# Weight sums of a block's first Strassen pass: accumulating DMAs in place of GpSimd adds, two operands with the other sign

## The chip, the cores and the metric

The kernel runs on one core of a Trainium2 chip. The metric is the device time of one execution in microseconds (us). Of the kernel before, three runs are at hand: 2923.96, 2926.63 and 2928.53 us, the median being 2926.63 us. The engines are called by the profile's names: PE (TensorE; PEld its weight loads), DVE (VectorE), ACT (ScalarE), POOL (GpSimd) and SP (SyncE, which issues DMAs).

## The reference, cut to what matters

One layer of a streaming encoder: an input projection, two token mixers (a gMLP chunk gate and a Mamba-2 SSD), and an output projection.

```python
def mixer_layer(x, ...):
    h = rms_norm(x, norm_in_w) @ w_in                 # 4096 (+64) tokens x 1024 @ 1024 x 5648
    u, v, g, z, xbc, dt_raw = jnp.split(h, SPLITS, axis=-1)
    a_out, vn = gmlp_branch(u, v, g, ...)
    b_out, h_last, new_conv = mamba_branch(z, xbc, dt_raw, ...)
    y = x + jnp.concatenate([a_out, b_out], axis=-1) @ w_out
```

The change concerns only the weights `w_in` of the first product, `h = norm(x) @ w_in`.

## The kernel before, in words

The 4096 tokens are worked through in blocks of 768 tokens (five of them, numbers 0 to 4) and a last block of 256 tokens with the 64 sample tokens. Blocks 0 to 4 compute the input projection by one level of Strassen's scheme (Winograd's form): a pair of 128-column slices of `w_in` is a unit, its 1024 x 256 weights are four quarters a11, a12 (one column slice, two halves of the rows) and a21, a22 (the other), and seven products q of combined quarters with combined activations give the unit's output. They are made in the order 1, 2, 4, 6, 7, 5, 3. Besides two v units (for v and dt) there are 18 units: c0 to c5 (for the convolution), then u0, g0, u1, g1, ... u3, g3, then z0 to z3, the last two interleaved.

Every operand of a product is split into a rounded part and a remainder (`hi` and `lo`), and three matmuls of each pair of 128-row tiles are summed, so a product is 12 matmuls of 384 columns (`products`, L1150 to L1152).

In block 0 the weight operands are made from the raw weights by `make`, written to DRAM (`wop_...`), and read back by `load` in blocks 1 to 4. So the sums of quarters are taken in block 0 alone. In `make(u, q, ts)`:

- L397, before product 1: a21 = a21 + a22.
- L403 and L404, every product: ACT copies the operand to `hi` (rounding), and DVE or POOL (`on_pool`: q = 4, 5, 3 of most units) takes `lo = src - hi`. L408 and L410 then send both to DRAM by SP's queue.
- L419, after product 1: a11 = a21 - a11, which is the operand of product 6.
- L421, after product 2: a12 = a12 - a11, the operand of product 3.
- L423, after product 4: a22 = a22 - a11, the operand of product 7.
- The operand of product 5 is a21.

These four sums are POOL instructions (128 x 512), save those of the units z2 and z3, which are DVE's; those of the two v units are DVE's (L412 to L414) and, for a12, POOL's (L415).

Raw weights lie in three buffers `wx`, one for (a11, a12) and one for (a21, a22) of a unit: `fetch` (L335) loads the second pair of the next unit early, and its first pair (a11, a12) into the buffer that is released when product 5 of the present unit has been made; the pair after that when product 3 has. Operands go to four buffers `w` that PE empties, so `ahead` runs up to four products ahead of PE. Each engine takes its instructions in the order that the scheduler of the program gave it, and each waits for semaphores.

`add_up` (L1159 on) adds each product into the four output quarters as it comes, on DVE, or on ACT where it only copies.

Between the projections of a block, its SSD steps, convolution and gates run on DVE, ACT and PE (`L910`, `L945`, `L1205` to `L1211` and others), on the same queues.

Of the kernel before, what the change touches and what calls it, by code (L numbers as in the profile page):

```python
# [10 lines left out]
AF = mybir.ActivationFunctionType  # L11
ALU = mybir.AluOpType
# [5 lines left out]
ADD, SUB = ALU.add, ALU.subtract  # L18
# [33 lines left out]
def hybrid_step_kernel(  # L52
# [30 lines left out]
    act, dve, pool, pe, sp = nc.scalar, nc.vector, nc.gpsimd, nc.tensor, nc.sync  # L83
# [44 lines left out]
    def phase1(p2):  # L128
# [141 lines left out]
        class Operands:  # L270
# [117 lines left out]
            def make(self, u, q, ts):  # L388


                v = u[0] == "v"
                n = 4 * WGD if v else 4 * P
                r = self.raw[u]

                eng = dve if u in (("z", 2), ("z", 3)) else pool
                if q == 1 and not v:
                    eng.tensor_tensor(r["a21"], r["a21"], r["a22"], ADD)  # L397
                src = r[{1: "a11", 2: "a12", 4: "a22", 6: "a11", 7: "a22", 5: "a21", 3: "a12"}[q]]
                if v:
                    hi, lo = ts  # L400
                else:
                    hi, lo = ts[0][:, :n], ts[0][:, n : 2 * n]
                act.copy(hi, src)  # L403
                (pool if q in self.on_pool[u[0]] else dve).tensor_tensor(lo, src, hi.bitcast(F32), SUB)  # L404
                k = ORDER.index(q)
                if v:
                    for i, x in enumerate((hi, lo)):
                        sp.dma_start(wops[u][(2 * k + i) * P : (2 * k + i + 1) * P, :], x.bitcast(F32))  # L408
                else:
                    sp.dma_start(wops[u][k * P : (k + 1) * P, :], ts[0][:, : 2 * n].bitcast(F32))  # L410
                if v and q == 4:
                    dve.tensor_tensor(r["a21"], r["a21"], r["a22"], ADD)  # L412
                    dve.tensor_tensor(r["a11"], r["a21"], r["a11"], SUB)
                    dve.tensor_tensor(r["a22"], r["a22"], r["a11"], SUB)  # L414
                    pool.tensor_tensor(r["a12"], r["a12"], r["a11"], SUB)  # L415
                elif v:
                    pass
                elif q == 1:
                    eng.tensor_tensor(r["a11"], r["a21"], r["a11"], SUB)  # L419
                elif q == 2:  # L420
                    eng.tensor_tensor(r["a12"], r["a12"], r["a11"], SUB)  # L421
                elif q == 4:
                    eng.tensor_tensor(r["a22"], r["a22"], r["a11"], SUB)  # L423
                if q in ((5, 3) if not v else (7, 5) if u[1] else (6, 7, 5)):
                    self.free += 1
                if q == 3:
                    del self.raw[u]
                self.fetch()
                return hi, lo
# [651 lines left out]
        class Strassen(Block):  # L1081
# [77 lines left out]
            def add_up(self, q, b, cs, hold=None):  # L1159

                c11, c12, c21, c22 = cs
                if q == 1:
                    act.copy(c12, b)
                elif q == 2:
                    dve.tensor_tensor(c11, b, c12, ADD)
                elif q == 4:
                    if hold is None:
                        act.copy(c21, b)
                    else:
                        hold.append(b)  # L1170
                elif q == 6:
                    dve.tensor_tensor(c12, b, c12, ADD)
                elif q == 7:
                    dve.tensor_tensor(c22, b, c12, ADD)  # L1174
                    dve.tensor_tensor(c21, hold.pop() if hold else c21, c22, ADD)
                elif q == 5:
                    dve.tensor_tensor(c22, b, c22, ADD)  # L1177
                    dve.tensor_tensor(c12, b, c12, ADD)
                else:
                    dve.tensor_tensor(c12, b, c12, ADD)  # L1180

# [679 lines left out]
```

## Time and profile before

| | |
|---|---|
| runs | 2923.96, 2926.63, 2928.53 us |
| the profiled execution | 2926.66 us, its span 2924.9 us |
| PE, PEld busy | 2800.6 us (96%), 2607.1 us (89%) |
| DVE, ACT, POOL busy | 2184.0 us (75%), 1283.8 us (44%), 670.2 us (23%) |
| granted TensorE clock, mean | 0.983 |
| DMA | 689.18 MB, mean 236 GB/s |

The span is the time from the first to the last instruction. Busy PE means that a matmul was under way. In a list of groups, a row is one kind of instruction: line, engine, operation, output<-input, shapes, count, then busy us and mean ns of one, then the idle time of that engine just before it and what ended it. In a timeline a row is: start in us, length in us, instruction, count, and in brackets the idle time before it and what ended that.

### The profile page before, as it was taken

Reading aid. Unit: us, or ns where it says so; the run is one execution under the profiler, and the core shown is the slowest. Engines: PE = TensorE matmul, PEld = TensorE weight load, DVE = VectorE, ACT = ScalarE, POOL = GpSimd, SP = SyncE. Lnnn points to the kernel's source line nnn. Section 1 sums busy time; section 2 is a strip of 40 time slices with the busy share of each in tenths; the row PEclk is TensorE's granted clock in tenths of the full one; section 3 lists DMA queues with packets and bytes.
Section 4 is the critical chain, followed back from the end, with each engine's and each line's share of the span. In section 5 each row is a group of like instructions: output and inputs, shape, how many; then the busy total and the mean of one; then the engine's idle time right before and its main releaser. Section 6 shows DMA issues by size and latency. Waiting matters only on the chain. (4 is left out here: it accounts for less than half of the span.)

```text
span 2924.9 us, 45556 instructions
## 1 busy us (share of the span) xinstructions
PE 2800.6 (96%) x16917; PEld 2607.1 (89%) x16917; DVE 2184.0 (75%) x3613; ACT 1283.8 (44%) x2415; POOL 670.2 (23%) x537
## 2 busy tenths in 40 slices
PE   5988998999999999999999999999999899989998
PEld 5887888999999999999999999999898688878886
DVE  7988888768757777676777666775666766698887
ACT  4366654245623365431664315663275222253332
POOL 1464443210012100031000211001311433353432
PEclk8998999999999999999999999999999899999999
DMA  8766777877788777886777877778776545544453
GB/s 284 270 243 228 248 281 282 305 229 236 243 312 278 233 235 245 285 309 218 253 243 266 288 252 238 235 251 281 232 257 224 160 163 171 173 158 166 166 173 112
DMA packets 310373, 689.18 MB, mean 236 GB/s; under 512 B 30264, under 2 KB 156936, under 8 KB 310152
## 3 DMA queue, kind: packets, MB, share of 16 engines
q1 hardware_dynamic: 309112, 686.26, 70.2%
q8 instruction: 135, 2.21, 0.3%
q14 instruction: 86, 0.70, 0.1%
q10 hardware_dynamic: 1040, 0.00, 0.0%
HBM read 535.43 MB, written 150.75 MB: 235 GB/s over the span
## 5 line engine op out<-in xcount | busy, mean ns | idle before, releaser
L1150 PE MATMUL mm<-hop,w 128*128 128x384 f32 x1656 | 577.8, 349 | 14.9 <-ACT w L403 6.9
L1152 PE MATMUL mm<-hop,w 128*128 128x384 f32 x1656 | 563.7, 340 | 11.8 <-POOL w L404 7.1
L1151 PE MATMUL mm<-hop,w 128*128 128x384 f32 x1656 | 563.0, 340 | 0.0
L1658 PE MATMUL pa<-wlo,oh 128*128 128x512 f32 (+1 forms) x928 | 366.3, 395 | 13.4 <-DVE wlo L1612 13.4
L1659 PE MATMUL pa<-whi,ol 128*128 128x512 f32 (+1 forms) x928 | 364.4, 393 | 3.5 <-DVE ol L1620 3.5
L1657 PE MATMUL pa<-whi,oh 128*128 128x512 f32 (+1 forms) x928 | 364.4, 393 | 2.6 <-ACT whi L1611 1.4
L1150 PEld LDWEIGHTS mm<-hop,w 128*128 128x128 f32 x1656 | 314.3, 190 | 24.0 <-ACT w L403 10.8
L1152 PEld LDWEIGHTS mm<-hop,w 128*128 128x128 f32 x1656 | 313.9, 190 | 16.5 <-POOL w L404 9.1
L1151 PEld LDWEIGHTS mm<-hop,w 128*128 128x128 f32 x1656 | 314.3, 190 | 4.0 <-issue 2.4
L1150 PE MATMUL mm<-hop,wy 128*128 128x384 f32 x864 | 297.0, 344 | 1.8 <-DVE arena L1174 1.8
L1151 PE MATMUL mm<-hop,wy 128*128 128x384 f32 x864 | 292.2, 338 | 0.0
L1152 PE MATMUL mm<-hop,wy 128*128 128x384 f32 x864 | 291.7, 338 | 0.0
L1658 PEld LDWEIGHTS pa<-wlo,oh 128*128 128x128 f32 (+1 forms) x928 | 174.3, 188 | 57.6 <-DVE wlo L1612 19.4
L1659 PEld LDWEIGHTS pa<-whi,ol 128*128 128x128 f32 (+1 forms) x928 | 174.7, 188 | 42.5 <-DVE ol L1620 4.2
L1657 PEld LDWEIGHTS pa<-whi,oh 128*128 128x128 f32 (+1 forms) x928 | 174.2, 188 | 42.2 <-ACT whi L1611 1.8
L1110 PE MATMUL mm<-w,hop 128*128 128x260 f32 x552 | 160.4, 292 | 14.4 <-ACT w L403 12.2
L910 ACT ACTIVATE acb<-acb,acu 128x128 f32<-128x128 f32 (+1 forms) x528 | 166.6, 389 | 0.6
L1150 PEld LDWEIGHTS mm<-hop,wy 128*128 128x128 f32 x864 | 162.4, 188 | 3.3 <-DVE arena L1174 2.4
L1151 PEld LDWEIGHTS mm<-hop,wy 128*128 128x128 f32 x864 | 162.5, 188 | 1.3
L1152 PEld LDWEIGHTS mm<-hop,wy 128*128 128x128 f32 x864 | 162.2, 188 | 0.3
L1112 PE MATMUL mm<-w,hop 128*128 128x260 f32 x552 | 158.1, 287 | 0.0
L1202 ACT ACTIVATE arena<-cvr,prm 128x768 f32<-128x768 f32 x60 | 61.5, 1027 | 192.6 <-DVE cvr L1177 152.9
(337 smaller groups left out, 6345.1 us busy)
## 6 DMA issues: line engine op xcount, KB each, us to landing
w<-wop_c SPq DMA_DIRECT2D x114, 512.0 KB, 4.3
w<-wop_v SPq DMA_DIRECT2D x84, 520.0 KB, 4.9
w<-wop_u SPq DMA_DIRECT2D x76, 512.0 KB, 4.3
w<-wop_g SPq DMA_DIRECT2D x76, 512.0 KB, 4.4
w<-wop_z SPq DMA_DIRECT2D x76, 512.0 KB, 5.3
wy<-wop_c SPq DMA_DIRECT2D x72, 512.0 KB, 4.4
acb<-acd SPq DMA_DIRECT2D x66, 512.0 KB, 5.3
raw<-ab SPq DMA_DIRECT2D x64, 512.0 KB, 4.4
```

The lines of the kernel that those rows point to most:

```text
L910: act.activation(M[:L, i, :L], M[:L, i, :L], AF.Relu, bias=self.acu[:L, ci, h0 + i : h0 + i + 1])
L1110: pe.matmul(pv, a, hi[:, j, :], start=(j == 0), stop=False)
L1112: pe.matmul(pv, b, hi[:, j, :], start=False, stop=(j == 3))
L1150: pe.matmul(b, hi[:, j, :], thi[:, j, :], start=j == 0, stop=False)
L1151: pe.matmul(b, hi[:, j, :], tlo[:, j, :], start=False, stop=False)
L1152: pe.matmul(b, lo[:, j, :], thi[:, j, :], start=False, stop=j == 3)
L1202: act.activation(o, raw[:, 3 : 3 + TS], AF.Identity, bias=prm[:, CB + c : CB + c + 1], scale=cw(3))
L1657: pe.matmul(b, x[0][:, j, :], hi, start=first, stop=False)
L1658: pe.matmul(b, x[0][:, j, :], lo, start=False, stop=False)
L1659: pe.matmul(b, x[1][:, j, :], hi, start=False, stop=last)
```

## The change

The sums of the 18 units become DMAs that POOL issues with an accumulation, `r[a] = r[a] + r[b]`, from SBUF to SBUF. Since such a DMA adds only, a21 + a22 is multiplied by -1 on ACT, in place, right after it is formed. Then a11 + a21 is the negative of what L419 made, so the operands of products 6 (a11) and 5 (a21) have the other sign, while a12 + a11 and a22 + a11 are what L421 and L423 made. `add_up` subtracts products 6 and 5. The v units take the same signs on DVE, and POOL's sum of theirs moves to DVE.

```diff
-                eng = dve if u in (("z", 2), ("z", 3)) else pool
+                add = lambda a, b: pool.dma_start(r[a], r[b], accum_op=ADD)
                 if q == 1 and not v:
-                    eng.tensor_tensor(r["a21"], r["a21"], r["a22"], ADD)
+                    add("a21", "a22")
+                    act.activation(r["a21"], r["a21"], AF.Copy, scale=-1.0)
...
                 if v and q == 4:
-                    dve.tensor_tensor(r["a21"], r["a21"], r["a22"], ADD)
-                    dve.tensor_tensor(r["a11"], r["a21"], r["a11"], SUB)
-                    dve.tensor_tensor(r["a22"], r["a22"], r["a11"], SUB)
-                    pool.tensor_tensor(r["a12"], r["a12"], r["a11"], SUB)
+                    dve.scalar_tensor_tensor(r["a21"], r["a21"], -1.0, r["a22"], ALU.mult, SUB)
+                    for a, b in (("a11", "a21"), ("a22", "a11"), ("a12", "a11")):
+                        dve.tensor_tensor(r[a], r[a], r[b], ADD)
                 elif v:
                     pass
                 elif q == 1:
-                    eng.tensor_tensor(r["a11"], r["a21"], r["a11"], SUB)
+                    add("a11", "a21")
                 elif q == 2:
-                    eng.tensor_tensor(r["a12"], r["a12"], r["a11"], SUB)
+                    add("a12", "a11")
                 elif q == 4:
-                    eng.tensor_tensor(r["a22"], r["a22"], r["a11"], SUB)
+                    add("a22", "a11")
...
                 elif q == 6:
-                    dve.tensor_tensor(c12, b, c12, ADD)
+                    dve.tensor_tensor(c12, c12, b, SUB)
...
                 elif q == 5:
-                    dve.tensor_tensor(c22, b, c22, ADD)
-                    dve.tensor_tensor(c12, b, c12, ADD)
+                    dve.tensor_tensor(c22, c22, b, SUB)
+                    dve.tensor_tensor(c12, c12, b, SUB)
```

In the changed kernel all four adds of a unit stand on L394, and lines after L415 are numbered one lower. The scheduler orders the instructions of each engine anew. Two places show it.

POOL's queue for the last convolution unit, c5, before (`wx_1891` holds a11 and a12, `wx_1751` a21 and a22 of c5; `wx_1916` holds a21 and a22 of the next unit):

```order
L419 TENSOR_TENSOR wx_1891<-wx_1751,wx_1891 128x512
L404 TENSOR_TENSOR w_1983<-wx_1751,w_1983 128x512
L421 TENSOR_TENSOR wx_1891<-wx_1891 128x512
L423 TENSOR_TENSOR wx_1751<-wx_1751,wx_1891 128x512
L397 TENSOR_TENSOR wx_1916<-wx_1916 128x512
L1212 COPY carp_145<-cvr_1847 128x3
```

and POOL's queue for the same unit in the changed kernel (`wx_1896` holds a11 and a12, `wx_1755` a21 and a22, `wx_1921` those of the next unit):

```order
L394 DMA wx_1896<-wx_1755 128x512
L404 TENSOR_TENSOR w_1989<-wx_1755,w_1989 128x512
L394 DMA wx_1921<-wx_1921 128x512
L394 DMA wx_1896<-wx_1896 128x512
L394 DMA wx_1755<-wx_1896 128x512
```

The a21 sum of the next unit has moved ahead of the a12 and a22 sums of the present one; those two wait for the landing of the first DMA, and the a22 sum is issued after the a12 sum.

ACT's queue in the changed kernel, around the copies for products 6, 7, 5 and 3 of unit c5 (L403 are the `hi` copies; L1201, L1212, L944, L1162 and L875 are other work of ACT):

```order
L1162 COPY cvr_2014<-mm_2018 128x384
L875 COPY bt_2245<-ss_2193 128x256
L403 CAST w_2009<-wx_1896 128x512
L944 ACTIVATE arena_155<-arena_155,prm_76 128x128 x2
L397 ACTIVATE wx_1921<-wx_1921 128x512
L403 CAST w_2031<-wx_1755 128x512
L403 CAST w_2052<-wx_1755 128x512
L1212 ACT_TABLE_LOAD
L1212 ACTIVATE arena_155<-arena_155 128x768
L403 CAST w_2075<-wx_1896 128x512
L1212 ACTIVATE arena_155<-arena_155 128x768
L1201 ACTIVATE arena_155<-cvr_2016,prm_76 128x768
```

The multiplication by -1 (L397) stands between the copies for products 6 and 7, so it is ahead of the copy that waits for the a22 sum.

## Rows read from the trace of the kernel before

**Rows 1.** Busy time by stretch: the 18 units of block 0, those of block 1.

```profile
core 0: us, PE busy (x) PEld busy (x) DVE busy (x) ACT busy (x) POOL busy (x), PEclk, DMA share, GB/s
103.70:501.60 397.90, 346.62 (x2014) 324.40 (x2013) 331.93 (x476) 227.19 (x426) 191.44 (x144) 0.95 0.71 253
566.40:884.60 318.20, 317.03 (x2005) 308.67 (x2003) 230.13 (x394) 154.75 (x301) 25.31 (x32) 1.00 0.78 258
```

**Rows 2.** Waits of ACT from 100 to 500 us: us in total, times, longest.

```profile
ACT w L403 <- DMA wx<-in_w_in_dram: 30.0, 7, 8.2
ACT w L403 <- POOL wx L423: 28.0, 8, 4.9
```

**Rows 3.** Timeline of POOL, unit c5.

```profile
210.02 1.68 POOL L419 TENSOR_TENSOR wx<-wx 128x512 f32<-128x512 f32 x1 [1.86 <-DVE w L404]
211.66 2.01 POOL L404 TENSOR_TENSOR w<-wx,w 128x512 fp32r<-128x512 f32 x1
...
215.33 2.01 POOL L423 TENSOR_TENSOR wx<-wx 128x512 f32<-128x512 f32 x1
```

**Rows 4.** Timeline of ACT and of SP's queue, unit c5 to the next.

```profile
208.62 1.64 ACT L403 CAST w<-wx 128x512 fp32r<-128x512 f32 x3
...
217.37 0.62 ACT L403 CAST w<-wx 128x512 fp32r<-128x512 f32 x1 [2.93 <-POOL wx L423]
...
229.11 1.64 ACT L403 CAST w<-wx 128x512 fp32r<-128x512 f32 x3
...
222.69 1.17 SPq L335 DMA_DIRECT2D wx<-in_w_in_dram  x1
```

**Rows 5.** Timeline of POOL and ACT in unit g0.

```profile
258.74 1.30 POOL L423 TENSOR_TENSOR wx<-wx 128x512 f32<-128x512 f32 x1
...
265.03 0.60 ACT L403 CAST w<-wx 128x512 fp32r<-128x512 f32 x1
```

**Rows 6.** Groups of POOL from 100 to 500 us (of four adds, the first and the last).

```profile
L404 POOL TENSOR_TENSOR w<-wx,w 128x512 fp32r<-128x512 f32 x49 | 78.5, 1606 | 98.9 <-ACT w L403 94.8 <-issue 3.5 <-POOL w L404 0.5
L423 POOL TENSOR_TENSOR wx<-wx 128x512 f32<-128x512 f32 x16 | 25.0, 1562 | 0.5
...
L397 POOL TENSOR_TENSOR wx<-wx 128x512 f32<-128x512 f32 x15 | 22.4, 1492 | 25.4 <-DMA wx<-in_w_in_dram 25.2
```

**Rows 7.** Groups of DVE from 100 to 500 us.

```profile
L404 DVE TENSOR_TENSOR w<-wx,w 128x512 fp32r<-128x512 f32 x73 | 64.9, 897 | 34.2 <-ACT w L403 33.7
L1211 DVE SCALAR_TENSOR_TENSOR arena<-cvr,prm,arena 128x768 f32<-128x768 f32 x12 | 18.1, 1509 | 0.1
L1017 DVE TENSOR_TENSOR S<-S,dte 128x512 f32<-128x512 f32 x12 | 13.1, 1090 | 0.0
L397 DVE TENSOR_TENSOR wx<-wx 128x512 f32<-128x512 f32 x2 | 2.5, 1231 | 0.0
```

**Rows 8.** Groups of DVE from 566 to 884 us, in block 1.

```profile
L1211 DVE SCALAR_TENSOR_TENSOR arena<-cvr,prm,arena 128x768 f32<-128x768 f32 x12 | 12.2, 1014 | 0.2
L1017 DVE TENSOR_TENSOR S<-S,dte 128x512 f32<-128x512 f32 x12 | 8.2, 683 | 0.0
```

**Rows 9.** Instructions on tile w, 100 to 500 us: duration in ns, min/median/max.

```profile
L403 ACT CAST w<-wx x122: 600/615/627, 99.5 to 486.7; 128x512 fp32r<-128x512 f32 x122
L404 DVE TENSOR_TENSOR w<-wx,w x73: 673/692/1939, 100.2 to 485.9; 128x512 fp32r<-128x512 f32 x73
L410 SPq DMA_DIRECT2D wop_c<-w x42: 319/320/1282, 100.9 to 224.3; - x42
```

**Rows 10.** DMAs from 100 to 500 us: packets; count, KB each, median us to landing.

```profile
DMA packets 58067, 101.36 MB, mean 253 GB/s; under 512 B 3096, under 2 KB 36984, under 8 KB 58038
...
wop_c<-w SPq DMA_DIRECT2D x42, 512.0 KB, 2.6
wx<-in_w_in_dram SPq DMA_DIRECT2D x32, 512.0 KB, 5.5
wop_u<-w SPq DMA_DIRECT2D x28, 512.0 KB, 3.5
```

## The prediction

> **What bounds the kernel now.** I read the busy time by stretch first. PE is busy nearly always over the whole span, so only a stretch in which it isn't can give time back. The 18 units of block 0 take 397.9 us for 2014 matmuls, those of block 1 318.2 us for 2005 [rows 1]: 80 us are lost in block 0, at a granted clock of 0.95 against 1.00. In the stretch that loses time the weight operands are made: ACT, DVE and POOL all have more to do, and POOL is busy 191 us instead of 25. The sums that the change moves lie there and nowhere else, so 80 us is all that it could win.
>
> Then the waits of ACT in that stretch. Its copies of operands wait 28.0 us in 8 units for POOL's a22 sum (L423), and 30.0 us in 7 units for raw weights [rows 2]. These waits form a cycle, which the timelines of unit c5 show: the copy for product 1 starts at 208.62, as soon as a11 and a12 have landed [rows 4]; POOL starts the a11 sum at 210.02 and ends the a22 sum at 217.34, with the remainder of product 4 and the a12 sum between [rows 3]; at 217.37 ACT copies for product 7 [rows 4]; product 5 releases the buffer, SP issues the next a11 and a12 at 222.69, and the next unit's first copy starts at 229.11 [rows 4]. That is 20.5 us per unit, of which POOL's link is 7.32 us. PE empties only four operands ahead of this.
>
> Not every unit hangs on that link. In g0 the a22 sum ends at 260.04 and its copy comes at 265.03 [rows 5]: 5.0 us of slack, since ACT's queue holds other work first.
>
> Last, the groups. POOL's four adds of a unit cost 25.0 to 22.4 us a group (four groups, about 95 us together), its remainders 78.5 us [rows 6]. DVE's instructions with two inputs in SBUF are slow beside them: 1509 and 1090 ns for forms that take 1014 and 683 ns in block 1 [rows 7, 8], and the remainder on DVE takes 897 ns in the mean where its median is 692 [rows 7, 9].
>
> **The change part by part.** The sum is made against the profiled execution, 2926.66 us (span 2924.9), which is the median of the runs (2926.63) to 0.03 us.
>
> *POOL's adds go.* DVE loses time to POOL of 73 x 0.205 = 15.0 us on the remainders, 12 x 0.495 = 5.9 us on L1211 and 12 x 0.407 = 4.9 us on L1017, 25.8 us in all [rows 7 to 9]. The adds are 95 of the 95 + 78.5 us in which POOL works on two such inputs [rows 6], so 55% of it, 14 us, goes. The remainders on POOL stay, and the rest of the delay with them. DVE's own eight adds for z2 and z3 go too: at 0.69 to 1.23 us each [rows 7, 9], 8 us. Against that stand two sums of the v units that POOL did and DVE now does, at about twice that form's length, 2.5 us. DVE gets 14 + 8 - 2.5 = 20 us back. Between 0 (all of it hidden under the cycle) and 20 us reach the path; I take half, **-10 us**, since ACT, DVE and POOL take turns in the cycle but much of DVE's work is beside it.
>
> *The DMAs come.* Let X be the time from POOL's issue of such a DMA to its landing and x what POOL spends on an issue. In place of POOL's link stand: a11 (X), the issue of a12 (x), a22 (X), so 2X + x; product 4's remainder and the next unit's a21 sum run on POOL during the first flight. No row shows an accumulating DMA. The nearest rows are stores of operands from SBUF: 512 KB landing after 2.6 and 3.5 us [rows 10]. The new ones move 256 KB but read source and destination, about as many bytes read. The lower end is 2.6, the upper the loads' 5.5 us [rows 10]. For x the ends are SP's issue, 0.32 us [rows 9], and a short POOL add, 1.3 us [rows 5]. I take X = 3.5 and x = 0.8, the longer store and the middle: 7.8 us for 7.32, +0.5 us in each of the 8 units that wait there, **+4 us**. In the ten others the slack of 5.0 us covers it. The link's ends are 5.5 us (-1.8 x 8 = -14 us) and 12.3 us (+5.0 x 8 = +40 us). POOL's link also waits now for ACT's multiplication, which was finished during the unit before.
>
> By the Trainium skill (DMA: Bandwidth & Descriptors, "Anatomy of one DMA - SWDGE (gpsimd) path") a DMA issued by GpSimd takes about 2.0 us plus its bytes over 436 GB/s, which estimates 2.6 us for 256 KB. With that as X the link would be 6.0 us and this term -10 us instead of +4. No run here shows it, and it counts neither the second read nor the traffic beside it, so it stays out of my sum.
>
> *The multiplication by -1 on ACT*: 18 x 0.615 us = 11 us at the length of a copy of that shape [rows 9]. It waits for the landing of the a21 sum, and behind it in ACT's queue stands the copy for product 7. That one waits for a DMA issued two issues later, so the cover is the a22 flight: **0**. Were the loads of a21 and a22 late, POOL would hold a12 and a22 behind the a21 sum, ACT the copy, and up to 11 us show.
>
> *The 16 DMA engines*: 72 DMAs of 256 KB are 18.9 MB beside 101.4 MB in the stretch [rows 10], at a busy share of 0.71 [rows 1]. The loads of a11 and a12, 5.5 us, are on every unit's cycle. I put 0.2 us on most of 18, **+3 us**; from 0 to 5.5 x 0.19 x 18 = 18 us if loads stretch as the bytes do.
>
> *The signs*: a subtraction instead of an addition of the same shapes in `add_up`: 0; it is the same DVE instruction.
>
> Sum: -10 + 4 + 0 + 3 = -3 us: 2923 us, **no change** by 0.2% (5.9 us), which is about what a measurement of this kernel can tell. This case by itself spans 2910 to 2935.
>
> **The rivals.**
>
> *Slower: the DMA's latency takes the place of POOL's add on the cycle.* Place: from the a11 sum to the copy for product 7, twice per unit. For it: two flights in series stand where four short adds stood, and loads take 5.5 us under this traffic. Against: stores take 2.6. With the relief of -10 and +3, 8 x (2X + 0.8 - 7.32) passes 7 us at X = 3.7 and makes the kernel slower by 0.2% at X = 4.1. At X = 5.5 and x = 1.3 it is +40 - 10 + 3 = +33: 2960 us. Chance 0.27.
>
> *Slower: the DMA engines become late.* For it: shares of 0.71 in the mean hide full stretches, and the loads are on the cycle. Against: block 1 runs at 0.78 without PE waiting [rows 1]. +18 in place of +3: 2939 us. Chance 0.10. The Trainium skill (the same page, "Issuing engines are not separate DMA queues") says that DMAs of all issuing engines share the same 16 engines; no run here shows it for POOL's.
>
> *Faster: flights are short and the relief is whole.* X = 2.6, x = 0.8: 8 x (6.0 - 7.32) = -10; relief -20: 2897 us. For it: 80 us are there to win and three engines crowd in that stretch. Against: the cycle's greater part, 13 us of load and copies, stays. Chance 0.20.
>
> *The change does not do what it says* would need the sums to stay on POOL; the order of its queue shows them as DMAs, so no chance.
>
> **How the numbers follow.** The forecast has 0.43, of which 0.22 lies within 5.9 us of 2926.66, 0.18 below, 0.03 above. Faster: 0.18 + most of 0.20 = 0.37. Same: 0.22 + 0.02 = 0.24. Slower: 0.03 + 0.27 + 0.10, less a little that ends inside = 0.39. The range runs from 2899, near the fast rival, to 2966, past the slow one; beyond lie X above 5.5 and the whole relief with the shortest flights.
>
> **What would show it.** Right: the 18 units of block 0 take about 395 us; POOL is busy about 95 us less there; L1211 falls from 1509 to about 1250 ns; the DMAs on L394 land after about 3.5 us. Wrong: ACT's copies wait for these DMAs by more than 28 us in total (the slow rival), the raw loads take over 6 us (the second), or the units come down to 370 us (the fast one).

## The result and the profile after

The changed kernel takes **3010.94 us** (median; 3004.34 to 3016.06), beside 2927.58 us for the kernel before on the same chip: ratio **1.0284, 95% interval 1.0271 to 1.0298**, 83 us slower. The forecast was 2923 us and its range ended at 2966. The profiled execution took 3016.06 us, with a span of 3014.4 us. In the changed kernel all four sums stand on L394 (the helper), the multiplication on L397, and lines behind L415 are one lower than before: L1210 is the former L1211, L1016 the former L1017.

Busy time by stretch, the units of block 0 and of block 1:

```profile
core 0: us, PE busy (x) PEld busy (x) DVE busy (x) ACT busy (x) POOL busy (x), PEclk, DMA share, GB/s
103.80:583.10 479.30, 370.48 (x2013) 342.54 (x2011) 294.61 (x461) 231.16 (x438) 147.61 (x151) 0.88 0.83 249
647.40:965.70 318.30, 317.98 (x2014) 309.73 (x2012) 228.36 (x393) 154.79 (x300) 24.77 (x31) 1.00 0.79 257
```

The units of block 0 take 479.3 us for 397.9 [rows 1], and block 1 takes what it took: the 81 us are all lost where the sums are made. PE is busy 370 us of the 479, so it waits.

The waits of ACT in those units (us in total, times, longest):

```profile
ACT w L403 <- DMA wx<-wx: 69.3, 18, 6.6
ACT wx L397 <- DMA wx<-wx: 40.9, 13, 13.4
ACT w L403 <- issue: 35.7, 10, 8.2
ACT w L403 <- DMA wx<-in_w_in_dram: 22.1, 6, 6.8
```

Where ACT's copies waited 28.0 us in 8 places for POOL's a22 sum [rows 2], they now wait 69.3 us in 18 for the new DMAs: 56 us ahead of copies for product 7 (a22) and 13 us ahead of copies for product 6 (a11). For another 35.7 us the profile names no releaser; before, it was 4.0 us. The copies wait less than before for raw weights: 22.1 us for 30.0.

POOL's timeline in unit c5 (start, duration, engine, line; in brackets the idle time before and its releaser):

```profile
211.01 0.87 POOL L394 DMA_DIRECT2D wx<-wx  x1 [3.86 <-DVE w L404]
211.62 1.58 POOL L404 TENSOR_TENSOR w<-wx,w 128x512 fp32r<-128x512 f32 x1
212.86 1.17 POOL L394 DMA_DIRECT2D wx<-wx  x1
...
217.56 1.73 POOL L394 DMA_DIRECT2D wx<-wx  x2 [3.33 <-DMA wx<-wx]
```

ACT's timeline in the same unit:

```profile
209.03 1.66 ACT L403 CAST w<-wx 128x512 fp32r<-128x512 f32 x3 [1.67 <-PE mm L1151]
...
217.32 0.62 ACT L403 CAST w<-wx 128x512 fp32r<-128x512 f32 x1 [4.10 <-DMA wx<-wx]
...
219.67 0.63 ACT L397 ACTIVATE wx<-wx 128x512 f32<-128x512 f32 x1 [0.40 <-DMA wx<-wx]
...
223.52 1.66 ACT L403 CAST w<-wx 128x512 fp32r<-128x512 f32 x3 [1.62 <-DMA wx<-wx]
```

SP's queue, the next raw load:

```profile
226.94 0.72 SPq L335 DMA_DIRECT2D wx<-in_w_in_dram  x1
```

Read it as a chain. POOL issues the a11 sum at 211.01; it lands 6 us later, and then two things go on: ACT copies for product 6 (217.32), and POOL issues a12 and a22 (217.56, two in one row). The a22 sum lands before 223.52, where ACT copies for product 7. From the a11 sum to that copy it is 12.5 us, where it was 7.35 [rows 3, 4], and the next raw load is issued 18 us behind the unit's first copy instead of 14.

In the unit before it, and in six others, there is more between the flights; POOL's timeline:

```profile
187.13 0.86 POOL L394 DMA_DIRECT2D wx<-wx  x1 [2.05 <-DVE dg L506]
187.69 1.59 POOL L404 TENSOR_TENSOR w<-wx,w 128x512 fp32r<-128x512 f32 x1
188.94 0.47 POOL L1211 COPY carp<-cvr 128x3 f32<-128x3 f32 x1
189.69 0.86 POOL L394 DMA_DIRECT2D wx<-wx  x1 [0.28 <-POOL carp L1211]
```

Here a remainder stands in POOL's queue between the a12 and the a22 issue, behind the a11 landing: 3.2 us from landing to the a22 issue instead of 1.0 to 1.3.

Groups of POOL, then of DVE, from 100 to 600 us (busy us, mean ns | idle before it):

```profile
L404 POOL TENSOR_TENSOR w<-wx,w 128x512 fp32r<-128x512 f32 x49 | 72.5, 1482 | 150.7 <-ACT w L403 150.7
L394 POOL DMA_DIRECT2D wx<-wx x68 | 62.8, 969 | 171.9 <-DVE w L404 76.1 <-DMA wx<-wx 51.4 <-DVE ea L982 10.1
...
L404 DVE TENSOR_TENSOR w<-wx,w 128x512 fp32r<-128x512 f32 x73 | 54.8, 761 | 133.1 <-ACT w L403 128.3 <-POOL carp L1211 2.7 <-issue 1.9
L1210 DVE SCALAR_TENSOR_TENSOR arena<-cvr,prm,arena 128x768 f32<-128x768 f32 x12 | 13.7, 1148 | 0.0
L1016 DVE TENSOR_TENSOR S<-S,dte 128x512 f32<-128x512 f32 x12 | 10.0, 831 | 0.0
```

DVE's relief came, and larger than forecast: the remainder takes 761 ns for 897, L1210 1148 for 1509, L1016 831 for 1090 [rows 7]. It stands beside 128 us in which DVE waits for ACT's copies.

DMA queues (packets, MB, share of the 16 engines) and median landings from 100 to 600 us:

```profile
q1 hardware_dynamic: 59556, 106.50, 61.2%
q0 software_dynamic: 10224, 18.62, 21.2%
...
wop_c<-w SPq DMA_DIRECT2D x42, 512.0 KB, 3.6
wx<-wx POOLq DMA_DIRECT2D x68, 256.0 KB, 5.6
wx<-in_w_in_dram SPq DMA_DIRECT2D x32, 512.0 KB, 5.8
```

All landings on L394 in the same stretch, from that line's instructions:

```profile
DMA to landing us min/median/max: 3.2/5.6/9.0
```

An accumulating DMA of 256 KB lands after 5.6 us in the median, as late as a raw load of 512 KB. q0, which carries only these, takes 21.2% of the engines' time for 18.62 MB, q1 61.2% for 106.50 MB: 1.98 times as much per MB.

### The profile page after: what moved, and what is told of

It reads as the page before. It is cut to its first block, busy times and chain, and to the rows that moved or that the text cites. A ratio compares the mean times of both kernels' runs of the same rounds, so it can differ in the third digit from the quotient of the medians.

```text
span 3014.4 us, 45699 instructions
## 1 busy us (share of the span) xinstructions
PE 2830.2 (94%) x16917; PEld 2631.0 (87%) x16917; DVE 2147.3 (71%) x3607; ACT 1289.9 (43%) x2429; POOL 612.9 (20%) x543
## 5 line engine op out<-in xcount | busy, mean ns | idle before, releaser
L1149 PE MATMUL mm<-hop,w 128*128 128x384 f32 x1656 | 588.7, 355 | 41.8 <-ACT w L403 34.1
L1151 PE MATMUL mm<-hop,w 128*128 128x384 f32 x1656 | 572.4, 346 | 9.3 <-POOL w L404 6.0
L1150 PE MATMUL mm<-hop,w 128*128 128x384 f32 x1656 | 570.8, 345 | 0.0
L1149 PEld LDWEIGHTS mm<-hop,w 128*128 128x128 f32 x1656 | 321.7, 194 | 52.9 <-ACT w L403 39.8
L1151 PEld LDWEIGHTS mm<-hop,w 128*128 128x128 f32 x1656 | 320.2, 193 | 15.9 <-POOL w L404 8.0
L1150 PEld LDWEIGHTS mm<-hop,w 128*128 128x128 f32 x1656 | 321.4, 194 | 4.0 <-issue 2.5
L1109 PE MATMUL mm<-w,hop 128*128 128x260 f32 x552 | 160.4, 292 | 14.3 <-ACT w L403 12.2
L404 DVE TENSOR_TENSOR w<-wx,w 128x512 fp32r<-128x512 f32 (+1 forms) x81 | 64.7, 808 | 134.2 <-ACT w L403 128.9
```

Source lines behind the costliest of these rows:

```text
L1109: pe.matmul(pv, a, hi[:, j, :], start=(j == 0), stop=False)
L1149: pe.matmul(b, hi[:, j, :], thi[:, j, :], start=j == 0, stop=False)
L1150: pe.matmul(b, hi[:, j, :], tlo[:, j, :], start=False, stop=False)
L1151: pe.matmul(b, lo[:, j, :], thi[:, j, :], start=False, stop=j == 3)
```

## The experiments

Three theories stood at the start. **Theory 1**: the flights are on the unit's cycle, so their latency sets the loss. **Theory 2**: the traffic of 72 more DMAs delays everything. **Theory 3**: ACT stands still behind its multiplication, which waits for a DMA. Every ratio is to the kernel before on the same chip; a difference in us is ratio - 1 times 2927.

One measure serves for all: the mean spacing in us of ACT's seven copies in a unit, worked out from the starts of its 126 casts of block 0 (the first 16 units; z2 and z3 are interleaved). A column is a step from the copy for one product to that for another. A flight (the time from a DMA's issue to its landing) of a11 stands between the copies for products 4 and 6, one of a22 between 6 and 7.

| kernel | 1 to 4 | 4 to 6 | 6 to 7 | 7 to 5 | 5 to 3 | 3 to next 1 | unit |
|---|---|---|---|---|---|---|---|
| before | 2.8 | 3.7 | 4.4 | 2.6 | 2.9 | 6.0 | 22.4 |
| changed | 2.9 | **7.0** | **7.4** | 1.7 | 2.5 | 5.7 | 27.2 |
| changed, without the multiplication | 2.5 | **6.1** | **8.2** | 1.6 | 2.0 | 6.5 | 27.0 |
| a21, a12 by DMA | 2.8 | 3.2 | 4.1 | 2.6 | 3.0 | 5.9 | 21.6 |
| a21, a12 by DMA, with the multiplication | 2.9 | 5.5 | 3.3 | 3.0 | 2.8 | 5.7 | 23.2 |
| a11 alone by DMA | 2.6 | **6.1** | 4.2 | 2.3 | 3.0 | 5.8 | 24.0 |
| a22 alone by DMA | 3.2 | 3.0 | **7.7** | 2.0 | 2.8 | 5.1 | 23.8 |
| delay on POOL, no DMA | 3.4 | 3.2 | **10.9** | 1.9 | 2.8 | 5.3 | 27.5 |

The changed kernel loses 3.3 + 3.0 us at the two flights and gets 1.6 back in the steps behind them: in all some 4.8 us per unit. In four of the 16 units its multiplication, too, stands ahead of the copy for product 6 and waits 27.9 us there; but without it the two steps together are as long (14.3 us for 14.4).

**Two sums off the cycle by DMA.** The kernel before with (`add` is the changed kernel's helper)

```
-                    eng.tensor_tensor(r["a21"], r["a21"], r["a22"], ADD)
+                    add("a21", "a22")
...
-                    eng.tensor_tensor(r["a11"], r["a21"], r["a11"], SUB)
+                    eng.tensor_tensor(r["a11"], r["a11"], r["a21"], SUB)
...
-                    eng.tensor_tensor(r["a12"], r["a12"], r["a11"], SUB)
+                    add("a12", "a11")
```

and the other signs that follow.

> The kernel before with two of a unit's four sums, a21 and a12, as accumulating DMAs issued by POOL, and a11 and a22 still added by POOL (a11 as a11 - a21, so that ACT multiplies nothing); 36 DMAs instead of 72, none between a unit's a11 sum and its copy for product 7. Theory 1 (two flights of 5.6 us stand in series on each unit's cycle): the link keeps two adds, a remainder and an issue, about as long as before, so the loss goes whole: 2915 to 2932 us. Theory 2 (the traffic of the DMAs on the 16 engines delays everything): half the bytes, half of the 83 us lost: about 2968 us. Theory 3 (ACT stands still in order behind its multiplication, which waits for a DMA: 40.9 us in 13 waits): that multiplication is gone, so 41 us come back: about 2970 us.

Measured: 2921.98 us, **0.9968 (0.9957 to 0.9979)**, faster than both kernels. The busy time in its units, by stretch:

```profile
105.20:494.20 389.00, 340.79 (x2013) 319.93 (x2012) 322.07 (x468) 227.38 (x426) 170.15 (x147) 0.96 0.87 283
```

DVE's groups in it, from 100 to 500 us:

```profile
L1212 DVE SCALAR_TENSOR_TENSOR arena<-cvr,prm,arena 128x768 f32<-128x768 f32 x12 | 15.8, 1320 | 0.1
L1018 DVE TENSOR_TENSOR S<-S,dte 128x512 f32<-128x512 f32 x12 | 11.0, 920 | 0.0
```

The units take 389.0 us for 397.9 although the DMA engines are at 0.87 instead of 0.71, more than the changed kernel's 0.83: theory 2 falls. L1212 and L1018 (before L1211 and L1017 [rows 7]) get half to two thirds of the relief that they get in the changed kernel; the remainder on DVE takes 873 ns, nearly the 897 of before.

**a11 alone stays on POOL.** As above, and a22 by DMA too:

```
-                    eng.tensor_tensor(r["a22"], r["a22"], r["a11"], SUB)
+                    add("a22", "a11")
```

> The kernel before with a21, a12 and a22 as accumulating DMAs and only a11 added by POOL (no multiplication on ACT); 54 DMAs, one flight on the cycle. Theory 1: the link is an add of 1.4, a remainder of 2.0, an issue of 1.0 and a flight of 5.6 us, 10 us in place of 7.3, so about 2.7 us in each of 18 units: +48 us, 2965 to 2980 us. Theory 2: three quarters of the bytes, +62 us: 2990 us. Theory 3: 2970 us, and the same as with a21 and a12 alone.

Measured: 2965.79 us, 1.0121 (1.0106 to 1.0136): one flight put on the cycle costs 45 us against the kernel just above, at the lower end of what theory 1 expected.

**a11 and a22 alone by DMA.** The changed kernel with

```
-                    add("a21", "a22")
+                    here("a21", "a22")
...
-                    add("a12", "a11")
+                    here("a12", "a11")
```

where `here` is the add on POOL (DVE for z2 and z3), as before.

> The changed kernel with only a11 and a22 as accumulating DMAs; a21 (with ACT's multiplication behind it) and a12 are added by POOL again. 36 DMAs, as many as with a21 and a12 alone, but both flights on the cycle. Theory 1: the link stays 2 x 5.6 + 1.3 us: 3000 to 3015 us. Theory 2: half the bytes, +41 us: 2968 us. Theory 3: the multiplication waits for an add of 1.3 us instead of a flight, 41 us come back: 2970 us.

Measured: 2989.58 us, 1.0202 (1.0185 to 1.0219), below theory 1's 3000 and above the others' 2970. 36 DMAs on the cycle cost 59 us where 36 off it gain 9, so the place decides and not the number. Of the 24 us that are missing to the changed kernel, the next run finds most.

**a22's DMA ahead of a12's.**

```
-                elif q == 2:
-                    add("a12", "a11")
                 elif q == 4:
                     add("a22", "a11")
+                    add("a12", "a11")
```

> The changed kernel with a unit's a22 DMA issued ahead of its a12 DMA instead of behind it. The same DMAs, bytes and multiplications. Theory 1: the link loses the a12 issue (0.97 us) and what the a12 transfer delays the a22 transfer in the queue (0 to 1.4 us): 18 x 1.0 to 2.4 = 17 to 43 us less than the changed kernel, 2968 to 2994 us. Theories 2 and 3: no difference, 3011 us.

Measured: 2992.25 us, 1.0211 (1.0192 to 1.0230): 21 us less than the changed kernel, within theory 1's range, for the same work in another order. The scheduler, which orders each engine's queue anew, put a22 first in eight of the first 16 units only, by issues, landings and the copies that follow. In these eight the a22 flight falls from 6.5 to 4.4 us in the mean, and the time from the a11 issue to the a22 landing from 13.3 to 10.3 us; in the other eight it is 16.4 us in both kernels. 8 x 3.0 = 24 us is about the 21 us won.

**A delay on POOL, without a DMA.** The kernel before with `PADS = 4` and, behind the a22 sum,

```
+                    for _ in range(PADS):
+                        pool.tensor_scalar(r["a22"], r["a22"], 1.0, None, ALU.mult)
```

> The kernel before, with no accumulating DMA at all, and four multiplications by 1.0 of a22 on POOL behind each unit's a22 sum: a pure delay D of the link, between four times 0.6 and four times 1.4 us, 2.4 to 5.6 us (the trace will give it). One flight lengthened the link by 2.7 us and cost 35 us, 13 us for each us. Theory 1 (what counts is the length of the link, whatever makes it): 13 to 17 us for each us of D, 2962 to 3020 us, all of it in block 0's units. Theory 2 (the DMAs' traffic): no DMA is added, 2930 us.

Measured: 3019.72 us, 1.0312 (1.0298 to 1.0326). POOL's group, from 100 to 590 us:

```profile
L426 POOL TENSOR_SCALAR wx<-wx 128x512 f32<-128x512 f32 x72 | 118.9, 1651 | 6.1 <-DVE wx L424 0.8
```

ACT's costliest wait in it (us in total, times, longest):

```profile
ACT w L404 <- POOL wx L426: 140.1, 18, 11.9
```

D is 4 x 1.65 = 6.6 us, more than the 2.4 to 5.6 expected, and 91 us / 6.6 = 13.8 us for each us of it: in theory 1's 13 to 17. A loss as large as the changed kernel's comes with no DMA at all. ACT waits in 18 units of 18. Nor does POOL's extra work slow DVE, which would be another cause: DVE's remainder takes 905 ns for 897 [rows 7].

**Half of a22 by DMA.** In the kernel with a11 alone on POOL:

```
-                    add("a22", "a11")
+                    h = 2 * P
+                    pool.dma_start(r["a22"][:, :h], r["a11"][:, :h], accum_op=ADD)
+                    pool.tensor_tensor(r["a22"][:, h:], r["a22"][:, h:], r["a11"][:, h:], ADD)
```

> The kernel with only a11 on POOL (2966 us, one flight on the cycle), with half of a22's columns summed by the DMA and the other half by POOL beside it: the flight moves 128 KB instead of 256. If the 5.6 us of a flight are its own bytes, it falls to 2.8 to 3.5 us and the link to 7.5 us: 2922 to 2935 us. If they are a fixed latency and the wait behind other transfers, it falls by at most 0.8 us: 2950 to 2966 us.

Measured: 2956.72 us, 1.0100 (1.0085 to 1.0116). Landings of the 128 KB DMAs in it:

```profile
DMA to landing us min/median/max: 3.6/5.7/8.5
```

In the mean of the first 16 units it is 6.0 us, where the whole quarter took 6.9: half the bytes take off 0.9 us. So most of a flight is not the time of its own bytes.

**POOL's a12 add behind its a22 add**, no DMA; and, with the same move of the line, **a12's DMA behind the a22 add** in the kernel with two DMAs:

```
-                elif q == 2:
-                    eng.tensor_tensor(r["a12"], r["a12"], r["a11"], SUB)
                 elif q == 4:
                     eng.tensor_tensor(r["a22"], r["a22"], r["a11"], SUB)
+                    eng.tensor_tensor(r["a12"], r["a12"], r["a11"], SUB)
```

> The kernel before, without any accumulating DMA, with POOL's a12 sum behind its a22 sum instead of ahead of it. Theory 1: the link loses an add of 1.4 us in each of 8 units: 11 us less, 2916 to 2920 us, where the kernel with the same order and two sums as DMAs gets DVE's relief besides. If it is as fast as that kernel, the DMAs bring nothing and the order all.

> The kernel with a21 and a12 alone as DMAs (2922 us), with a12's DMA issued behind POOL's a22 add instead of ahead of it. Theory 1: the link loses an issue of 1.0 us in each unit that waits for it (8 of 18 before): 8 to 18 us less, 2904 to 2914 us; a12's flight has the copies for products 7 and 5 as cover. If no unit waits for POOL's link any longer: 2922 us.

Measured: 2930.03 us, 0.9999 (0.9987 to 1.0010), where 2916 to 2920 was expected, and 2920.90 us, 0.9974 (0.9965 to 0.9984), which is the 2922 us of the kernel without the new order. Neither tests the length of the link, because the move of the line hardly reached POOL's queue. In the first kernel the scheduler put the a12 sum (L422) ahead of the a22 sum (L421) again in 17 of 18 units. POOL's timeline of unit c5 in it:

```profile
208.62 1.68 POOL L419 TENSOR_TENSOR wx<-wx 128x512 f32<-128x512 f32 x1 [1.86 <-DVE w L404]
210.26 2.00 POOL L404 TENSOR_TENSOR w<-wx,w 128x512 fp32r<-128x512 f32 x1
212.23 1.74 POOL L422 TENSOR_TENSOR wx<-wx 128x512 f32<-128x512 f32 x1
213.93 2.01 POOL L421 TENSOR_TENSOR wx<-wx 128x512 f32<-128x512 f32 x1
```

From the a11 sum's start to the a22 sum's end the median of the first 16 units takes 8.0 us there as before, and 7.5 us in the second kernel as without the move; there only c1's link is clearly shorter, 3.4 us for 4.6.

The kernel with two sums by DMA does have a shorter link. POOL's timeline of unit c5 in that kernel (L420 is the a11 sum, L424 the a22 sum):

```profile
209.38 1.67 POOL L420 TENSOR_TENSOR wx<-wx 128x512 f32<-128x512 f32 x1 [1.87 <-DVE w L405]
211.01 2.01 POOL L405 TENSOR_TENSOR w<-wx,w 128x512 fp32r<-128x512 f32 x1
212.97 0.89 POOL L396 DMA_DIRECT2D wx<-wx  x1
213.59 1.61 POOL L424 TENSOR_TENSOR wx<-wx 128x512 f32<-128x512 f32 x1
```

An issue of 0.89 us stands where the a12 sum of 1.74 us stood, and the link takes 5.8 us for 7.3 [rows 3]; in the mean of 16 units it is 7.33 for 8.06 us. ACT's copies wait less for its end than the 28.0 us of before [rows 2]:

```profile
ACT w L404 <- POOL wx L424: 11.5, 5, 3.9
```

So the 9 us won by two DMAs may come from the shorter link as well as from DVE's relief, and no run here tells the two apart.

**a12 alone by DMA.**

```
-                    eng.tensor_tensor(r["a12"], r["a12"], r["a11"], SUB)
+                    add("a12", "a11")
```

> The kernel before with a12's sum alone as an accumulating DMA; a21, a11 and a22 are added by POOL. 18 DMAs, none on the cycle. If the gain of the kernel with a21 and a12 as DMAs (9 us) is DVE's relief from POOL's adds, half of it: 2924 to 2927 us. If it is the shorter link, all of it: 2921 us.

Measured: 2923.53 us, 0.9986 (0.9977 to 0.9995): 4 us, half of the gain with half of the DMAs. The interval, 2920.4 to 2925.7 us, holds the shorter link's 2921 and most of the relief's 2924 to 2927, so this run doesn't decide either.

**Without the four sums.**

```
-                if q == 1 and not v:
-                    eng.tensor_tensor(r["a21"], r["a21"], r["a22"], ADD)
...
-                elif q == 1:
-                    eng.tensor_tensor(r["a11"], r["a21"], r["a11"], SUB)
-                elif q == 2:
-                    eng.tensor_tensor(r["a12"], r["a12"], r["a11"], SUB)
-                elif q == 4:
-                    eng.tensor_tensor(r["a22"], r["a22"], r["a11"], SUB)
```

> The kernel before without the four sums of the 18 units: it leaves them out, so that the operands of these units are the raw quarters. It bounds what any way of making the sums can win. Theory 1: the link has no sums, and POOL and DVE are relieved of all of them; since a link 1.4 us shorter won nothing, the relief is most of it: 2900 to 2918 us. If POOL's link still set the pace of the 8 units that wait for it: 8 x 5 = 40 us and the relief, 2870 to 2885 us.

Measured: 2882.62 us, 0.9845 (0.9832 to 0.9859): leaving all four sums out wins 45 us, where the prediction put 80. That is the second figure of the expectation, so POOL's link still cost time in the kernel before, beside the relief. The first figure leaned on "a link 1.4 us shorter won nothing", which the run with the moved line had not shown.

**The multiplication taken out.**

```
-                    act.activation(r["a21"], r["a21"], AF.Copy, scale=-1.0)
```

> The changed kernel without ACT's multiplication of a21 by -1; it leaves the sign out, so that a11, a22 and a12 get a21 + a22 with the other sign. All 72 DMAs stay where they are. Theory 3 (ACT stands in order behind its multiplication): the 40.9 us of 13 waits and 11 us of work go, 2960 to 2975 us. Theory 1 (flights on the cycle): the cycle has no multiplication in it, so at most its 0.6 us of ACT in each unit, 3000 to 3011 us. The run with a11 and a22 alone as DMAs, 22 us under the changed kernel, had ACT wait as long before the multiplication (42.2 us in 12 waits, for POOL's add), which speaks against theory 3.

Measured: 3010.54 us, 1.0276 (1.0261 to 1.0290), as the changed kernel: with two flights on the cycle, theory 3 is worth nothing, though the profile names 40.9 us for it.

**a22 on POOL, a11 by DMA.** The changed kernel with

```
-                    add("a22", "a11")
+                    here("a22", "a11")
```

> The changed kernel with a22 added by POOL again (DVE for z2 and z3); a21 with its multiplication, a11 and a12 as DMAs: 54 DMAs and one flight on the cycle, as in the kernel with only a11 on POOL (2966 us), from which it differs in which flight is on the cycle and in having ACT's multiplication. Theory 1: a flight of 5.6, an issue of 1.0 and an add of 1.4 to 2.0 us, 8 to 8.6 us for 7.3: 18 x 0.7 to 1.3 us = +13 to +24 over the kernel without DMAs on the cycle (2922), 2935 to 2966 us. Theory 3: the multiplication's 41 us on top of the 2966 us: about 3005 us.

Measured: 2962.27 us, 1.0115 (1.0097 to 1.0132). In the range of theory 1, but at its upper end, and with a link of only 9.3 us in the median of 16 units, 1.3 more than before. Four more runs asked whether the a11 flight (**A**) or the multiplication (**B**) costs it: the kernel just named without the multiplication; with the a11 sum on POOL as well,

```
-                    add("a11", "a21")
+                    here("a11", "a21")
```

and kernels with one flight and no other DMA.

> The kernel with a21, a11 and a12 as DMAs and a22 on POOL (2962 us) without ACT's multiplication by -1; it leaves the sign out. Theory A (the a11 flight by itself): 2955 to 2966 us. Theory B (the multiplication, which waited 42.7 us there): 2920 to 2935 us.

> The changed kernel with a11 and a22 added by POOL: a21 and a12 as DMAs, ACT's multiplication behind the a21 DMA, no flight between a11's sum and the copy for product 7. It differs from the kernel with the same two DMAs (2922 us) by the multiplication alone. Theory A: 2920 to 2932 us. Theory B: 2950 to 2962 us.

> a11's sum alone as a DMA, the three others on POOL, no multiplication; it leaves the sign out. Theory A: one flight of 4.6 to 5.7 us in place of an add of 1.5, on the cycle through the copy for product 6: 2950 to 2966 us. Theory B: no multiplication, 2925 to 2935 us. If the DMAs of a21 and a12 add to the flight's cost, it is at the lower end.

> The kernel before with a22's sum alone as a DMA, the three others on POOL, no multiplication. With a21 and a12 as DMAs besides it was 2966 us. Theory A: the flight alone, 2955 to 2970 us. If the DMAs off the cycle delay the flight, 2940 to 2955 us.

Measured: without the multiplication 2956.76 us, 1.0083 (1.0067 to 1.0099); both on POOL 2945.19 us, 1.0041 (1.0026 to 1.0056); a11 alone 2957.80 us, 1.0085 (1.0068 to 1.0102); a22 alone 2952.31 us, 1.0067 (1.0052 to 1.0082).

So A holds: one flight alone costs 25 us (a11) or 20 us (a22), with no multiplication. For a22 the time lies below A's 2955 and in the range for a flight that other DMAs had delayed before. B is true where no flight is on the cycle: there the multiplication costs 0.0041 + 0.0032, 21 us, and the time lies between A's 2932 and B's 2950. (The two kernels also differ in the v units' sums, which move to DVE.) The wait for it, in that kernel's waits of ACT:

```profile
ACT wx L399 <- DMA wx<-wx: 47.5, 11, 9.3
```

And one instance, in its timeline of ACT:

```profile
161.26 0.63 ACT L399 ACTIVATE wx<-wx 128x512 f32<-128x512 f32 x1 [5.28 <-DMA wx<-wx]
161.79 0.60 ACT L405 CAST w<-wx 128x512 fp32r<-128x512 f32 x1
```

ACT, in order, waits 5.28 us for the landing of the next unit's a21 sum, and the copy for product 6 stands behind. This is the step from 4 to 6 in the table, 5.5 us for 3.2: in five of the first 16 units the multiplication stands ahead of that copy and waits 27.8 us in all; in six it stands ahead of the copy for product 5 (9.0 us). With one flight the multiplication costs 9 us (1.0115 against 1.0083; the intervals just overlap), with two nothing: the same ACT is waiting anyway. Landings of the a22 DMAs where they are the only ones:

```profile
DMA to landing us min/median/max: 3.3/4.7/7.8
```

The median is 4.7 us, and 6.4 us with a21 and a12 as DMAs beside it, where it costs 45 us instead of 20: the transfers issued ahead of it on its own queue lengthen it, as the eight units with a22 ahead of a12 showed.

## Why the prediction was wrong

*What bounds the kernel* was right as a place: block 0's units, and in them the cycle of ACT's copies with the sums in it. All of the change is there. The bound of 80 us was loose: without any sum 45 us are won.

*POOL's adds go, -10 us.* The relief came, and L1210 at 1148 ns is below the 1250 that was named as a sign. What it is worth in time has no run of its own. Two DMAs off the cycle win 9 us and a12's alone 4, but with half of the sums moved, or a quarter, and with POOL's link 0.7 us shorter besides; that the 9 us lie near the 10 is in part luck. POOL's busy time fell by 44 us and not 95 (191.4 to 147.6), since 68 issues at 0.97 us count as POOL's too.

*The DMAs come, +4 us.* This is the step that failed, in two of its terms.

First X. "I take X = 3.5", from the longer store of operands; measured 5.6, least 3.2. The upper bound, the loads' 5.5, was the fitting row. The link was to be 2X + x; with the measured X and x it would be 2 x 5.6 + 0.97 = 12.2 us. From the a11 issue to the a22 landing, it is 14.8 us in the mean of the first 16 units, where the same span on POOL took 8.1: the a22 flight is 6.6 us behind a12's transfer, and in seven units a remainder stands between the flights, which the prediction had put beside the first.

Second the count, "8 units that wait there", and "In the ten others the slack of 5.0 us covers it". A link 6.7 us longer is past that slack: the prediction's own count would give 8 x 6.7 + 10 x 1.7 = 71 us. With -10 and +3 that is +64, where +83 was measured. The copies' spacing shows one reason why that is short: the prediction priced only the a22 end of the link, yet the a11 flight holds up the copy for product 6 by itself, and a11 alone costs 25 us. The trace of the kernel before already had copies that wait for the a11 sum, from 100 to 500 us, which the prediction left out:

```profile
ACT w L403 <- POOL wx L419: 8.7, 5, 3.3
```

So the slow rival's mechanism is what happened, "the DMA's latency takes the place of POOL's add on the cycle", and its X of 5.5 was right. Its price of +40 was not, since it kept the 8 units. By its own rule, slower from X = 4.1 on, the outcome was decided.

*The multiplication, 0.* Right in effect: taking it out changes nothing here, as its cover by flights would have it; without flights on the cycle it costs 21 us. But the copy for product 7 stands behind it in eight of the first 16 units only, and in four it is the copy for product 6.

*The 16 DMA engines, +3 us.* Raw loads take 5.8 for 5.5 us, stores of wop_c 3.6 for 2.6 [rows 10]. Where the flights are off the cycle, engines 0.87 busy cost nothing that shows: that kernel is faster.

How the 83 us come together, from the runs: a11's flight alone 25, a22's alone 20, with both and the multiplication 59, and 24 more with a21 and a12 as DMAs, of which putting a12 behind a22 (in half of the units) gives 21 back. The gap between 45 and 59 has no run of its own.

The Trainium skill (DMA: Bandwidth & Descriptors, "Anatomy of one DMA - SWDGE (gpsimd) path") gave 2.6 us as an estimate for X. The traces show 3.2 at the least and 5.6 in the median, so the measurement decides: its fit is no price for a DMA under this traffic. The same section of the Trainium skill gives a fixed part of about 2.0 us and a part that goes with the bytes; half of 256 KB would take off an estimated 0.3 us by it. The trace agrees that the part of the bytes is the small one, with 0.9 us off 6.9.

## What to carry to other kernels

Before work moves from an engine to a DMA, ask of each piece whether its successor waits for it: 36 such DMAs gained 9 us off the cycle and cost 59 on it. Price a flight by the slowest DMA in the same stretch of the trace, not by the quickest, and let every copy that reads its result count, not the last one alone. If one must be on the path, issue it ahead of those that nobody waits for. And when an experiment moves a line, look in the trace whether the queue's order moved with it: here it did in half of the units of one run, and in 1 of 18 of another.

## What was not expected of the hardware

An accumulating DMA from SBUF to SBUF takes about twice the engines' time per MB of the other DMAs here (21.2% for 18.62 MB, 61.2% for 106.50 MB). In the kernel with a22 alone by DMA it is 5.3% for 4.72 MB and 72.0% for 125.48 MB, 1.96 times. The Trainium skill (Collectives: The Full Stack, "The bandwidth ceiling: the fold count and why AG ≠ RS ≠ AR") says of a ReduceScatter that its add in the DMA reads two sources and so doubles the read traffic; the trace's 1.98 agrees. No run here has a plain DMA from SBUF to SBUF, so it isn't shown that the add is the cause, nor which side of a transfer is the slow one.

An in-place multiplication of one operand by a constant took POOL 1.65 us (L426), no less than its adds of two, 1.45 to 1.63 us there.

In block 0's units of the changed kernel PE's busy time grew as well, 346.6 to 370.5 us for the same number of matmuls, with the granted clock at 0.88 for 0.95. Both are means over stretches at the levels of 2.4 and 1.2 GHz. In the second of these two stretches PE mostly waited, and its granted clock was 0.64:

```profile
260.00:270.00 10.00, 9.99 (x69) 9.54 (x70) 8.49 (x10) 3.13 (x6) 5.62 (x6) 1.00 0.96 278
270.00:280.00 10.00, 3.09 (x12) 2.56 (x11) 4.88 (x8) 5.51 (x10) 2.99 (x2) 0.64 0.66 190
```

The kernel with the delay and no DMA has the same, 369.9 us at 0.87, so it comes with the waiting and not with the DMAs. How much of the loss it makes is not shown. ACT's copies don't wait longer for PE than before: 16.6 us in 12 places for 22.2 in 9.
